# Last output projection on float16 pairs: splits of gated tiles spread over several heads, one stored group per weight block, second half left to the scheduler

## The chip, the cores and the metric

The kernel runs on one core of a Trainium2 chip. The metric is the device time of one execution in microseconds (us), the median of several runs. The engines named here are PE (TensorE, the matrix engine; PEld is its weight load), DVE (VectorE), ACT (ScalarE), POOL (GpSimd) and SP (SyncE, which issues most transfers). Each engine works through its own instruction stream in order; semaphores hold an instruction back until what it needs is there. [...]

## The reference

One step of a streaming encoder of two layers, over 512 prompt tokens and 32 sample tokens (544 rows in all, width 1024). Layer 0 is an RWKV-7 mixer, layer 1 is differential attention with 12 heads; each layer has a gate of 2048 columns and an output projection of 2048 by 1024.

```
h = rmsnorm(x, norm_w)
q, k, v, qm, gate = jnp.split(h @ w_in, [MIX_W, 2 * MIX_W, 3 * MIX_W, 3 * MIX_W + MEM_W], axis=-1)
...                                             # 12 heads of differential attention: o
o = rmsnorm(o, subln) * (1.0 - lam_init)
y_mem = mem_attention(qm, mk, mv)
out = jnp.concatenate([o.reshape(B, T, MIX_W), y_mem], axis=-1) * jax.nn.silu(gate)
return x + out @ w_out, k, v
...
y = rmsnorm(x, final_norm_w)                    # after layer 1
```

Besides `y`, the kernel returns the keys and values of layer 1 and the states of layer 0. The change touches layer 1 alone: the last heads of its attention, and `out @ w_out`.

## The kernel before, in words

Layer 0 takes roughly the first 1000 us and is left as it is. Layer 1 runs one long stream of matrix products on PE. Its unit is a **block**: 128 output columns of a weight matrix, 1024 rows deep. The activations are held as 8 or 16 **tiles** of 128 channels by 544 tokens. A weight block and the activations are both split into a pair of float16 numbers (high part and rest), and a product is the sum of high by high, high by rest and rest by high. A block is thus 2 token halves of 272 by 8 tiles by 3 products: 48 matrix products. The code counts one **step** per product.

**Heads.** The blocks of head h are v, k, q and, for most heads, a gate block; head 11 has four gate blocks. The rest of the attention (scores, softmax, transposes, gating) is a list `ev` of calls in `diff_layer`, each tied to a step number `begin(h) + offset`; when the stream has yielded that many steps, the call is made and its instructions are put in the streams of the engines. The trace places the first steps of heads 8, 9, 10 and 11 at about 1113, 1141, 1162 and 1184 us and the first step of the output projection at 1248.8 us.

**Output projection.** `out` is 16 tiles deep, in two halves. The first 8 blocks (q=0) multiply tiles 0 to 7 by the 8 column blocks of `w_out`; the next 8 blocks (q=1) multiply tiles 8 to 15 and add to the same result. Tiles 0 to 7 are gated during the heads up to 8; tiles 8 to 15 are gated last (tiles 12 to 15 belong to the memory heads). Before a tile can be used it needs a **square** (`gated_square`: ACT squares it and sums along the tokens), then for the whole half a **scale** (`gated_scales`: one small PE product, `ps_gs`, and some DVE work that turns each bound into a power of two), `half_scale` (DVE, the scales that go onto the rows of `w_out`), and a **split** (`gated_split`: ACT writes the high part of `hl`, then DVE the rest).

**Weight blocks.** A weight block passes through a pipeline that `stream` (L1942) places within the steps of the blocks ahead of it. During the products of block i: two loads of 256 KB for block i+4 at steps 1 and 14 (SP issues them; there are four raw buffers `h16s`, so a load waits until the block four before it has been split); two squares of block i+3 on ACT at steps 14 and 27; the column scale of block i+2 at steps 12 to 36 (PE, DVE, then two multiplications on POOL); the split of block i+1 at steps 7, 11, 13 and 17 (ACT casts the high part into `whs`, then POOL subtracts for the first half and DVE for the second). `whs` has two buffers.

**Stored groups.** The attention's keys and values are written to a scratch array in DRAM. Six **groups** (`kv_out`) copy it to the outputs, 1 MB and 64 KB each, DRAM to DRAM, issued by SP. Before, while the first half of the projection runs, a list `left` is worked off one entry every 12 steps: 8 squares, the scales, `half_scale`, 8 splits of tiles 8 to 15; and then, when it is empty, one stored group every 12 steps, at steps 312 to 372 of 768.

**Order.** While `ordered` is set, every instruction is tied behind the one before it on its engine, so the order in the code is the order in the streams. At step 384, when the first half ends, `ordered` is cleared: the Tile scheduler then orders the instructions of the engines by itself, but for those in `tied`, before PE and SP.

**Result.** The sum of a second-half block is added to `x` (`out_add`, L1934). Then the final norm needs a sum of squares over all columns per token (`sums`, `ps_n`), and a transpose of each 128 by 128 piece on PE (`ps_f`) before the rows are stored; the last of this can only be done after the last product.

## Time and profile before

| what | us |
|---|---|
| median of 3 runs (lowest to highest) | 1384.32 (1384.22 to 1386.17) |
| profiled execution | 1382.54 |
| its span (first to last instruction) | 1380.7 |
| first product of the output projection | 1248.8 |
| last product ends | 1369.9 |

The profile is of one execution; every engine's instructions stand in it with start, length and what they waited for. Nearly all instructions are recorded in one helper, so they all bear its line (L133 before, L137 after the change, since four lines are added above it); they are told apart by the names of tiles. A row of a timeline gives the start, the length, the engine, the operation, output and inputs, the shape, a count, and in brackets the idle time of the engine just before and what ended it. A table by windows gives for each stretch the busy time of each engine, the granted PE clock (1.00 is full speed), the mean busy share of the DMA engines, and GB/s. The prediction shows the rows that it uses.

### The profile page before, as it was taken

The page shows a single profiled execution, that of the slowest core. Times are in us where ns is not written, and L with a number is a line of the kernel's source. Part 1 is how long each engine was busy: PE and PEld are TensorE (multiplying, and loading weights), DVE is VectorE, ACT ScalarE, POOL GpSimd, SP SyncE. Part 2 cuts the span into 40 slices and gives each one's busy share as a digit, 9 for nine tenths or more (in the row PEclk, how much of TensorE's full clock was granted, in tenths as well). Part 3 has the DMA queues.
Part 4 walks back from the last instruction along what each step waited for, and adds up shares of the span by engine and source line. Part 5 has one row for each costly group of instructions (what it writes and reads, how often), then busy time and mean ns, then how long its engine had stood idle before and what let it go on. Part 6 is the DMA issues. An engine that isn't in the chain of part 4 may idle for free. (4 is left out here: it accounts for less than half of the span.)

```text
span 1380.7 us, 32358 instructions
## 1 busy us (share of the span) xinstructions
PE 1305.1 (95%) x11775; PEld 1174.1 (85%) x11775; DVE 946.2 (69%) x2475; ACT 888.8 (64%) x2412; POOL 674.0 (49%) x1145
## 2 busy tenths in 40 slices
PE   6999999999999999899999999999999999989776
PEld 6898899999999999888899988888878877868665
DVE  7776777788778777856764464566796679767444
ACT  7665678677877786655643366776766767865442
POOL 2227575557655765540120047565566655535441
PEclk9999999999999999999999999999999999999989
DMA  7542223322332223233284446777777878743711
GB/s 235 176 129 71 67 56 89 97 61 67 93 87 69 72 78 81 58 101 117 60 265 151 129 123 156 184 165 178 171 179 151 185 154 183 162 109 93 254 48 66
DMA packets 418298, 171.55 MB, mean 124 GB/s; under 512 B 195209, under 2 KB 402578, under 8 KB 418138
## 3 DMA queue, kind: packets, MB, share of 16 engines
q1 hardware_dynamic: 417994, 168.96, 47.4%
q8 instruction: 93, 1.52, 0.5%
q14 instruction: 67, 0.55, 0.1%
q10 hardware_dynamic: 144, 0.52, 0.1%
HBM read 130.84 MB, written 41.92 MB: 125 GB/s over the span
## 5 line engine op out<-in xcount | busy, mean ns | idle before, releaser
L133 PEld LDWEIGHTS <-whs 128*128 128x128 f16 x3456 | 330.3, 99 | 85.9 <-ACT whs L133 11.6
L133 PE MATMUL ps_g<-h,whs 128*128 128x272 f16 x2688 | 335.1, 281 | 4.4 <-POOL whs L133 4.4
L133 PE MATMUL ps_g<-hh,wlo 128*128 128x272 f32 x912 | 277.8, 305 | 1.3 <-DVE wlo L133 1.3
L133 PE MATMUL ps_g<-hh,whi 128*128 128x272 f32 x912 | 275.2, 302 | 0.8 <-ACT hh L133 0.8
L133 PE MATMUL ps_g<-hl,whi 128*128 128x272 f32 x912 | 271.4, 298 | 0.6 <-POOL hl L596 0.5
L885 POOL TENSOR_TENSOR tm<-u,m 102x84 f32<-102x84 f32 (+23 forms) x372 | 152.8, 411 | 168.6 <-DMA m<-sc 140.6
L133 POOL TENSOR_TENSOR whs<-h16s,whs 128x512 f16<-128x512 f32 x128 | 150.7, 1195 | 72.2 <-ACT whs L133 70.5
L133 PEld LDWEIGHTS ps_g<-hh,whi 128*128 128x128 f32 x912 | 174.8, 192 | 4.3 <-ACT hh L133 1.2
L133 PEld LDWEIGHTS ps_g<-hh,wlo 128*128 128x128 f32 x912 | 174.0, 191 | 4.6 <-DVE wlo L133 1.9
L133 PEld LDWEIGHTS ps_g<-hl,whi 128*128 128x128 f32 x912 | 174.2, 191 | 2.4 <-POOL hl L596 0.7
L887 POOL TENSOR_TENSOR u<-u,tm 102x84 f32<-102x84 f32 (+23 forms) x372 | 160.0, 430 | 29.1
L133 DVE TENSOR_TENSOR wlo<-raw,whi 128x512 fp32r<-128x512 f32 x178 | 129.3, 736 | 47.7 <-ACT whi L133 46.6
L133 ACT CAST whi<-raw 128x512 fp32r<-128x512 f32 x178 | 107.0, 616 | 35.4 <-issue 19.3
L133 POOL TENSOR_SCALAR h16s<-h16s 128x512 f32<-128x512 f32 x112 | 78.8, 715 | 98.5 <-DVE h16s L133 92.5
L133 PE MATMUL ps_g<-hl,whs 128*128 128x272 f16 x768 | 94.9, 283 | 12.1 <-ACT whs L133 11.3
L133 ACT CAST whs<-h16s 128x512 f16<-128x512 f32 x144 | 84.1, 618 | 31.9 <-POOL h16s L133 26.5
L133 ACT ACTIVATE junkw<-h16s 128x512 bf16<-128x512 f32 x138 | 86.5, 627 | 22.7 <-DMA h16s<-in_w_out_dram 19.5
L133 DVE SCALAR_TENSOR_TENSOR SB<-ps_c,dl,sd 64x64 f32<-64x64 f32 x168 | 47.4, 282 | 42.6 <-PE ps_c L133 38.6
L133 PE MATMUL ps_g<-lo,whi 128*128 128x272 f32 x256 | 73.9, 289 | 0.7 <-DVE lo L133 0.7
L133 PE MATMUL ps_g<-hi,whi 128*128 128x272 f32 x256 | 73.7, 288 | 0.0
L133 PE MATMUL ps_g<-hi,wlo 128*128 128x272 f32 x256 | 73.6, 288 | 0.0
L133 ACT COPY sv<-ps_c 64x64 f32<-64x64 f32 x192 | 39.2, 204 | 38.8 <-PE ps_c L133 36.9
(413 smaller groups left out, 2931.5 us busy)
## 6 DMA issues: line engine op xcount, KB each, us to landing
raw<-in_rw_in_dram SPq DMA_DIRECT2D x114, 256.0 KB
h16s<-in_df_in_dram SPq DMA_DIRECT2D x112, 256.0 KB
raw<-in_w_out_dram SPq DMA_DIRECT2D x32, 256.0 KB
h16s<-in_w_out_dram SPq DMA_DIRECT2D x32, 256.0 KB
ptr<-pk SPq DMA_DIRECT2D x44, 160.0 KB
aT<-ptr SPq DMA_DIRECT2D x11, 640.0 KB
scr<-sg SPq DMA_DIRECT2D x96, 68.0 KB
out_dram<-scr SPq DMA_DIRECT2D x6, 1024.0 KB
```

The lines of the kernel that those rows point to most:

```text
L133: return lambda *a, **k: self.trunk.tie(self, issue(*a, **k))
L885: nc.gpsimd.tensor_tensor(tm[:, :n, :wd], u3[:, :n, kx : kx + 1].to_broadcast(sh), m3[:, kx : kx + 1, kx + 1 :].to_broadcast(sh), ALU.mult)
L887: nc.gpsimd.tensor_tensor(u3[:, :n, kx + 1 :], u3[:, :n, kx + 1 :], tm[:, :n, :wd], ALU.add)
```

## The change

Three things change, all in layer 1.

**Gated tiles 0 to 7.** Before, their squares stood at heads 10 and 11, the scales at step 60 of head 11, and their splits in head 11, with ACT's and DVE's part issued together. Now the squares stand from head 8 to head 10, the scales come in two groups of four (at heads 9 and 10), and the splits stand from step 37 of head 10 on. The rest (DVE's part) is a call of its own, `gated_rest`, 11 steps behind the cast.

**Gated tiles 8 to 15 and the stored groups.** The list in the projection's first half now gives each entry a step of its own. Squares are due from step 24 every 12 steps, but the loop that looks at the list starts at about step 93, so the first six squares are made at once. The scales are due at 126 (they were made at 192), the splits every 24 steps from 150 (they stood every 12 steps from 216), each rest 10 steps later, and the six stored groups every 48 steps, one block, from 164 to 404.

**The second half's order.** `tied` keeps SP alone: PE's order after step 384 is now the scheduler's too.

```diff
+GSQUARE = ((8, 36), (8, 132), (9, 36), (9, 84), (10, 2), (10, 29), (10, 53), (10, 75))
+GSCALE = ((9, 132), (10, 92))
+KVOUT = 164
+GSPLIT, GREST = (37, 66, 84, 115, 134, 180, 227, 252), 11
...
-        x, s = self.o1[g][:], self.out["s"][:, g : g + 1]
-        self.ae.activation(both[:, 0], x, AF.Copy, scale=s)
-        self.ve.scalar_tensor_tensor(both[:, 1], x, s, both[:, 0], ALU.mult, ALU.subtract)
+        self.ae.activation(both[:, 0], self.o1[g][:], AF.Copy, scale=self.out["s"][:, g : g + 1])
         tiles[g] = both[:, 0], both[:, 1]
+
+    def gated_rest(self, g, tiles):
+        hi, lo = tiles[g]
+        self.ve.scalar_tensor_tensor(lo, self.o1[g][:], self.out["s"][:, g : g + 1], hi, ALU.mult, ALU.subtract)
...
-            left = [(self.gated_square, (12, 13, 14, 15, 8, 9, 10, 11)), (lambda g: self.gated_scales(8, 8), (8,)), (self.half_scale, (1,)),
-                    (lambda g: self.gated_split(g, po, tiles), (12, 13, 14, 15, 8, 9, 10, 11))]
-            left = [(fn, g) for fn, gs in left for g in gs]
+            order = (12, 13, 14, 15, 8, 9, 10, 11)
+            left = [(24 + 12 * i, self.gated_square, g) for i, g in enumerate(order)]
+            left += [(126, lambda g: self.gated_scales(g, 8), 8), (138, self.half_scale, 1)]
+            left += [(150 + 24 * i, lambda g: self.gated_split(g, po, tiles), g) for i, g in enumerate(order)]
+            left += [(160 + 24 * i, lambda g: self.gated_rest(g, tiles), g) for i, g in enumerate(order)]
+            left += [(KVOUT + 48 * i, lambda i: kv_out[i](), i) for i in range(len(kv_out))]
+            left.sort(key=lambda x: x[0])
             for _ in main:
                 n += 1
-                if n % 12 == 0:
-                    if left:
-                        fn, g = left.pop(0)
-                        fn(g)
-                    elif kv_out:
-                        kv_out.pop(0)()
+                while left and left[0][0] <= n:
+                    _, fn, g = left.pop(0)
+                    fn(g)
                 if n == KT * 6 * KT:
-                    self.ordered, self.tied = False, (self.te, self.se)
+                    self.ordered, self.tied = False, (self.se,)
...
-            if h >= 10:
-                at(f + 36, lambda h=h: [self.gated_square(g) for g in ((0, 1), (6, 7))[h - 10]])
-                at(f + 66, lambda h=h: [self.gated_square(g) for g in ((2, 3, 4, 5), ())[h - 10]])
-                if last:
-                    at(f + 60, lambda: self.gated_scales(0, 8))
-                    at(f + 70, lambda: self.half_scale(0))
-                    for g in range(8):
-                        at(f + (84, 104, 124, 144, 184, 226, 260, 296)[g], lambda g=g: self.gated_split(g, we[0], tiles))
+                for g, off in enumerate(GSPLIT):
+                    at(f + off, lambda g=g: self.gated_split(g, we[0], tiles))
+                    at(f + off + GREST, lambda g=g: self.gated_rest(g, tiles))
+        for g, (h, off) in enumerate(GSQUARE):
+            at(begin(h) + off, lambda g=g: self.gated_square(g))
+        for g, (h, off) in zip((0, 4), GSCALE):
+            at(begin(h) + off, lambda g=g: self.gated_scales(g, 4))
+        at(begin(11) + 40, lambda: self.half_scale(0))
```

On SP, in the first half of the output projection (`h16s` is half a weight block, `scr` a group's scratch with its two transfers): before,

```order
L133 DMA h16s<-in_w_out_dram 128x4x128 x20
L133 DMA out_dram<-scr_12366 512x512
L133 DMA out_dram<-scr_12366 32x512
L133 DMA out_dram<-scr_12367 512x512
L133 DMA out_dram<-scr_12367 32x512
L133 DMA out_dram<-scr_14354 512x512
L133 DMA out_dram<-scr_14354 32x512
L133 DMA h16s<-in_w_out_dram 128x4x128
L133 DMA out_dram<-scr_14355 512x512
```

and now

```order
L137 DMA h16s<-in_w_out_dram 128x4x128 x14
L137 DMA out_dram<-scr_12366 512x512
L137 DMA out_dram<-scr_12366 32x512
L137 DMA h16s<-in_w_out_dram 128x4x128 x2
L137 DMA out_dram<-scr_12367 512x512
L137 DMA out_dram<-scr_12367 32x512
L137 DMA h16s<-in_w_out_dram 128x4x128 x2
L137 DMA out_dram<-scr_14354 512x512
```

Three groups stood in a row ahead of half a block, and the other three followed with single halves between them; now each group has the two halves of one block behind it.

On ACT, around the third block of the projection (`junkw` from `og` is the square of a gated tile, `whs` the cast of a weight block): before,

```order
L133 ACTIVATE junkw_18711,outt_12363<-og12_12341 128x544
L133 CAST whs_18713<-h16s_11842 128x512
L1874 DMA fw_18704<-in_final_norm_w_dram 128x1024
L133 ACTIVATE junkw_18729,outt_12363<-og13_12342 128x544
L133 CAST whs_18713<-h16s_11842 128x512
L133 ACTIVATE junkw_18739,h16s_11842<-h16s_11842 128x512
L133 ACTIVATE junkw_18752,outt_12363<-og14_12343 128x544
```

and now

```order
L137 ACTIVATE junkw_18712,outt_12363<-og12_12341 128x544
L137 ACTIVATE junkw_18714,outt_12363<-og13_12342 128x544
L137 ACTIVATE junkw_18716,outt_12363<-og14_12343 128x544
L137 ACTIVATE junkw_18718,outt_12363<-og15_12344 128x544
L137 ACTIVATE junkw_18720,outt_12363<-og8_12337 128x544
L137 ACTIVATE junkw_18722,outt_12363<-og9_12338 128x544
L137 ACTIVATE junkw_18727,outt_12363<-og10_12339 128x544
L137 CAST whs_18729<-h16s_11842 128x512
L1881 DMA fw_18708<-in_final_norm_w_dram 128x1024
L137 ACTIVATE junkw_18745,outt_12363<-og11_12340 128x544
L137 CAST whs_18729<-h16s_11842 128x512
```

Seven squares now stand ahead of the first cast of that block, where one stood, and the last square stands ahead of the second cast; the small product `ps_gs` needs all eight.

On DVE, in head 11 (`qp` is the query, `hl` the rest of a gated tile, `snm` the maximum of a row of scores, `pt` the softmax, `ot` the head's output): before,

```order
L133 STREAM_TRANSPOSE pk<-pt 128x512
L133 SCALAR_TENSOR_TENSOR qp<-ps_g,h16s,qp 64x272 x2
L133 SCALAR_TENSOR_TENSOR hl_18001<-og_12332,outs,hl_18001 128x544
L133 TENSOR_SCALAR h16s<-dv,h16s 128x1
L133 TENSOR_TENSOR ot<-ps_o,os_16826 128x512
L133 MEMSET ps_s 64x64 x2
L133 TENSOR_REDUCE snm<-ps_s 128x1 x2
```

and now

```order
L137 STREAM_TRANSPOSE pk<-pt 128x512
L137 SCALAR_TENSOR_TENSOR qp<-ps_g,h16s,qp 64x272 x2
L137 TENSOR_SCALAR h16s<-dv,h16s 128x1
L137 TENSOR_TENSOR ot<-ps_o,os_16830 128x512
L137 MEMSET ps_s 64x64 x2
L137 TENSOR_REDUCE snm<-ps_s 128x1 x2
```

The rest of a gated tile no longer stands between the query and the head's output there.

On PE the small products `ps_gs` move with the scales, and in the second half of the projection the transposes `ps_f` move. After block 11, twenty of them stood in a row; now they stand as groups of 8, 4, 4 and 4 (8, then 4 products, 4, then 1, 4, then 4, 4). In the last three token halves, two groups of 6 transposes and one of 2 stood between the products, the one of 2 with the first norm products (`ps_n`) ahead of the last 48 products. Now they stand as 4, 2, 2, 4 and 2 with 2 to 31 products between them, and the first `ps_n` stand ahead of the last 37 products. After the last product, three `ps_n` and then six `ps_f` remained before; now, six `ps_f` and then three `ps_n`.

## The prediction

> **What bounds the kernel now.** I read the page first, for the span, then the busy times by windows over layer 1's end, then PE's waits there, then SP's transfers and the chain of waits through the longest wait. The page gives

> ```profile
> span 1380.7 us, 32358 instructions
> ```

> against an execution of 1382.54 us, so 1.84 us lie outside the span. The windows cover the output projection (columns: window, its length, busy us of PE, PEld, DVE, ACT and POOL with counts, PE clock, DMA share, GB/s):

> ```profile
> 1249.00:1303.00 54.00, 53.25 (x486) 44.53 (x483) 38.69 (x94) 31.48 (x77) 29.55 (x26) 1.00 0.53 166
> 1303.00:1314.00 11.00, 0.00 (x0) 0.00 (x0) 0.00 (x0) 2.63 (x8) 0.00 (x0) 0.65 0.71 228
> 1314.00:1321.00 7.00, 6.31 (x34) 4.13 (x35) 2.61 (x7) 2.53 (x8) 3.19 (x3) 0.58 0.27 77
> 1321.00:1370.00 49.00, 41.69 (x362) 34.04 (x360) 26.38 (x69) 16.21 (x36) 17.75 (x16) 1.00 0.13 44
> 1370.00:1380.70 10.70, 1.51 (x12) 1.30 (x12) 4.52 (x14) 2.48 (x4) 0.00 (x0) 0.71 0.32 112
> ```

> PE is full in the first half, then has no product at all for 11 us, then runs at a clock of 0.58, then is short of 7.3 us of work in the last 49. PE's waits from 1184 on (what waited, for what; us in total, times, longest) say on whom:

> ```profile
> PE ps_sc L133 <- ACT pt L133: 3.1, 1, 3.1
> PE ps_aT L133 <- DVE pt L133: 2.1, 2, 1.8
> PE ps_aT L133 <- DVE os L133: 1.3, 1, 1.3
> ...
> PE ps_g L133 <- ACT whs L133: 11.3, 1, 11.3
> ...
> PE ps_n L133 <- DVE sums L133: 3.3, 2, 1.7
> PE ps_f L133 <- DVE og L133: 2.9, 2, 1.7
> PE ps_f L133 <- DVE h16s L133: 1.6, 1, 1.6
> PE ps_f L133 <- DVE x L133: 0.9, 2, 0.5
> PE ps_g L133 <- POOL whs L133: 0.8, 2, 0.6
> ```

> The long one names a cast on ACT. ACT itself waited, for a weight load, and the chain of waits leads past that load to the stored groups:

> ```profile
> 1312.05 0.63 ACT L133 ACTIVATE junkw<-h16s 128x512 bf16<-128x512 f32 x1 [6.67 <-DMA h16s<-in_w_out_dram]
> ```

> ```profile
> 1291.71 12.40 DMA out_dram<-scr
> 1304.18 8.61 DMA h16s<-in_w_out_dram
> ...
> 1315.84 4.32 DMA h16s<-in_w_out_dram
> ...
> 1323.45 3.23 DMA h16s<-in_w_out_dram
> ...
> 1329.74 3.18 DMA h16s<-in_w_out_dram
> ```

> SP's timeline shows the six groups as 12 transfers, the first here, and the last before 1302.24:

> ```profile
> 1285.24 5.10 SPq L133 DMA_DIRECT2D out_dram<-scr  x6
> ...
> 1302.24 13.97 SPq L133 DMA_DIRECT2D h16s<-in_w_out_dram  x4
> ```

> So the groups run from 1285.24 to 1304.1 almost without a pause. With two halves of a block among them that is 6 x 1.114 MB + 0.52 MB = 7.2 MB in 18.9 us, an estimated 2.9 us for a group. The weight load of 1304.18 waited behind all of it; PE used up what it had and stood still. That is the bound that the change meets.

> **The change part by part.** A step's length first:

> ```profile
> 1264.10 2.94 PE L133 MATMUL ps_g<-hl,whs 128*128 128x272 f16 x24
> 1266.88 0.19 PE L133 MATMUL ps_g<-h16s 128*128 128x1 bf16 x2
> 1266.93 2.94 PE L133 MATMUL ps_g<-hl,whs 128*128 128x272 f16 x24
> ```

> 24 products per 2.83 us, 0.118 us a step, 5.66 us a block.

> (1) **Groups spread.** One group per block puts 0.52 + 1.11 MB into 5.66 us, 289 GB/s, where the burst moved 7.2 MB in 18.9 us, 380. A load is issued when the split of the block four before it is done (step 17 at the latest) and is squared in the next block from step 14 on; less the time of the split itself some 80 steps lie between, 9.4 us. A load of 3.2 to 4.3 us with a group of 2.9 us ahead of it lands after 6.1 to 7.2. It is hidden. The 11.3 us go, and the slow clock behind them: 6.31 us busy at 0.58 lose 6.31 x 0.42 = 2.65. Against it stands the loop that the second half runs once the scheduler orders it (the square of a later block is put ahead of a cast, so load, square, cast and subtraction follow each other): from 1315.84 to 1323.45 and to 1329.74 it took 7.6 and 6.3 us, more than a block. Four loops of 6.3 lose 2.5; I estimate 0.5 in hand at its start, and 0.8 is waited already (the last row of the waits): +1.2. Sum -12.75, from -14 (no loop) to -7 (two loads late by a group each).

> (2) **Transposes after block 11.** Twenty stood in a row and waited 1.6 + 2.9 = 4.5 us on a chain through DVE, POOL and ACT that the change leaves. Between the first and the last of them now stand 9 products, 9 x 0.118 = 1.06. I take -1.1, nearest to what PE has to put in; ends 0 and -4.5.

> (3) **The last blocks.** The two waits on x (0.9) and the earlier of the two on sums (3.3 - 1.7 = 1.6) now have products ahead of them: up to -2.5. I take -2.0, since the last ones are released late anyhow; ends 0 and -2.5. What follows the last product, 10.7 us, stays.

> (4) **Head 11.** Here the head's output waited behind the rest of a gated tile:

> ```profile
> 1212.01 1.31 DVE L133 SCALAR_TENSOR_TENSOR hl<-og,outs,hl 128x544 f16<-128x544 f32 x1
> ...
> 1213.47 0.69 DVE L133 TENSOR_TENSOR ot<-ps_o,os 128x512 f32<-128x512 f32 x1
> ```

> ```profile
> 1212.00:1216.00 4.00, 0.91 (x37) 0.70 (x36) 3.45 (x8) 1.81 (x7) 0.73 (x1) 1.00 0.88 137
> 1216.00:1220.00 4.00, 2.23 (x13) 1.39 (x12) 3.05 (x10) 2.22 (x9) 1.36 (x2) 0.68 0.89 218
> 1220.00:1224.00 4.00, 4.00 (x21) 2.96 (x20) 0.83 (x5) 2.58 (x9) 2.27 (x2) 0.50 1.09 278
> ```

> Without that 1.31 the wait on pt falls from 3.1 to 1.8, and the next (1.8) by perhaps 0.1: -1.4. Between the two waits the clock fell: 2.23 x 0.32 + 4.00 x 0.50 = 2.7 us lost. With less idle time I expect no fall: -4.1 in all. Ends: 0, the chain is late for another reason; -7.6, both waits gone too.
> [...]

> (5) **The wait on os** (1.3) had a split's rest ahead of it on DVE too, and no split stands there now: -1.0; ends 0 and -1.3.

> (6) **Heads 8 to 10** take the work over. The squares and splits of head 10 (last two rows: all splits of the projection, ns shortest/median/longest):

> ```profile
> 1162.00:1184.00 22.00, 21.28 (x182) 18.38 (x183) 16.64 (x48) 18.30 (x52) 10.94 (x11) 1.00 0.62 139
> ```

> ```profile
> 1261.16 0.64 ACT L133 ACTIVATE junkw<-og 128x544 bf16<-128x544 f32 x1
> 1261.71 0.19 ACT L133 ACTIVATION_READ_ACCUMULATOR junkw<-og 128x1 bf16 x1
> ```

> ```profile
> L133 ACT ACTIVATE hl<-og,outs x16: 732/740/762, 1198.1 to 1288.7; 128x544 f16<-128x544 f32 x16
> L133 DVE SCALAR_TENSOR_TENSOR hl<-og,outs,hl x16: 769/785/1306, 1198.9 to 1289.5; 128x544 f16<-128x544 f32 x16
> ```

> A square takes 0.74 us. Head 10 loses two squares and gains five splits: ACT 18.30 - 1.5 + 3.7 = 20.5 of 22 us, DVE 16.64 + 3.9 = 20.6. PE is full there (21.28 of 22), and ACT and DVE feed it: this work is hidden behind its products as long as both keep ahead, and what they deliver late PE waits for. I take +1.0; ends 0 and +4 (five casts of 0.74 all in the way).

> (7) **A new wait.** `ps_gs` now stands at step 126 and needs all eight squares, which are issued together. On ACT one ended at 1261.9; six more at 0.74, the cast of a weight block (0.53 until the next starts) and the last square end at about 1267.6. PE reaches step 126 some 18 products after the mark of 1264.05, at 1266.2. In-order, PE's products queue behind it: +1.4, ends 0 and +3 (the row it is nearest to is this count itself). The weight cast behind seven squares is late by up to 5, too, but its products come after the wait.

> (8) **Splits of tiles 8 to 15** stand one per 24 steps instead of 12, 0.74 + 0.79 us each, ahead of the weight casts of four blocks: +0.5, ends 0 and +1.5 (one split for each pair of blocks).

> Sum: -12.75 - 1.1 - 2.0 - 4.1 - 1.0 + 1.0 + 1.4 + 0.5 = -18.05. The profiled execution becomes 1364.5, and with the 1.8 by which the median lies above it, **1366.3 us**.

> **The rivals.**
> Better cover: the loop never lags, the transposes and the last waits vanish, and `ps_gs` finds its squares ready. (1) -14, (2) -4.5, (3) -2.5, no (7): -24.6, **1359.7**. For it: every one of these waits is on a chain that runs ahead of PE. Against: 9 products don't cover 4.5 us.
> Head 11 stays: its wait comes from the softmax, and the clock falls as before; (4) is 0: **1370.4**. For it: 1.8 us of the first wait are not explained by the split. Against: the rest is exactly one instruction in order.
> The stall is ACT's order, not the groups: the square that waits at 1312.05 stands ahead of the cast in either kernel. If it keeps the cast back without any burst, (1) is 0: **1379.1**. Against: its load waited 8.61 us where 3.2 is usual, just behind the burst.
> Slower: each of six weight blocks waits for its group. PE would wait 2.9 us six times and lose some 2.7 us of clock each time as in head 11, 33.6 in all: -18.05 + 33.6, **1399.9**. It decides if a load lands more than 9.4 us after its issue; 6.1 to 7.2 by the rows speak against it.
> No effect: the scheduler puts the second half back as it was, and the loads are late for another reason: **1384**.

> **How the numbers follow.** Forecast 47%, better cover 17%, head 11 stays 22%, ACT's order 6%, slower 5%, no effect 3%. A measurement of this kernel tells about 0.2% (2.8 us) from no change, so the first four are faster: 0.92; same 0.03; slower 0.05. The forecast's own range is 1361 to 1371. Head 11's case lies in it, and better cover takes the low end to 1357; (6) and (7) at their upper ends add 4.6 to the case with head 11: 1375. Outside lie the last three cases and tails of the others, 2 in 10.

> **What would show it.** (1) SP alternates groups and pairs of halves, no wait on whs above 1 us near the border, clock 1.00 throughout; wrong if ACT's square before the second half's casts still waits for a load. (2), (3) waits of `ps_f` near 3.4 in all, and one `ps_n` wait, at the end. (4) `ps_sc` waits 1.8 us and the clock stays at 1.00. (6) new waits on ACT or DVE between 1113 and 1184. (7) `ps_gs` waits for `junkw`, 1 to 2 us. The prediction is wrong if the groups' transfers lengthen loads beyond 9 us, or if head 10's full engines cost PE more than (4) and (5) bring.

## The result, and the profile after

The changed kernel takes 1365.55 us (median of 4 runs, 1361.0 to 1367.86) against 1385.24 before (4 runs beside them): a ratio of 0.985 (0.982 to 0.989), 19.7 us. A second set of executions gave 1364.33 against 1384.88. The forecast was 1366.3.

The profiled execution took 1367.86 us, with a span of 1366.0, 14.7 us below the span before. PE's waits in the changed kernel, first for the heads (1095 to 1249 us), then from there to 1300, then to the end (what waited for what; us in total, times, longest):

```profile
PE ps_s L137 <- ACT pt L137: 2.3, 1, 2.3
PE ps_s L137 <- DMA kh<-kh: 2.1, 1, 2.1
PE ps_oT L137 <- DVE og L137: 1.7, 1, 1.7
PE ps_aT L137 <- DVE pt L137: 1.1, 1, 1.1
...
PE ps_gs L137 <- ACT junkw L137: 0.6, 1, 0.6
...
PE ps_g L137 <- POOL whs L137: 2.2, 3, 0.8
PE ps_f L137 <- DVE og L137: 2.0, 2, 1.2
PE ps_f L137 <- DVE h16s L137: 1.4, 1, 1.4
PE ps_g L137 <- ACT whs L137: 1.0, 1, 1.0
PE ps_n L137 <- DVE sums L137: 0.5, 1, 0.5
PE ps_f L137 <- DVE x L137: 0.5, 2, 0.3
```

The wait of 11.3 us for a cast is down to 1.0, with 2.2 beside it for POOL's part. Of head 11's waits the ones on scores (`ps_sc`, 3.1) and on os (1.3) are gone, and the one of `ps_aT` on `pt` is 1.1 where it was 1.8. The `ps_gs` wait that was forecast is there with 0.6. New are 2.3 us in head 11's first block and 1.7 in head 10's. SP's timeline shows the groups between the halves of weight blocks:

```profile
1267.87 1.25 SPq L137 DMA_DIRECT2D out_dram<-scr  x2
1271.99 1.56 SPq L137 DMA_DIRECT2D h16s<-in_w_out_dram  x2
1273.60 1.17 SPq L137 DMA_DIRECT2D out_dram<-scr  x2
1278.41 1.40 SPq L137 DMA_DIRECT2D h16s<-in_w_out_dram  x2
```

A table that a single profile's waits can't give was worked out from the starts of PE's products in each trace: how long PE took for stretches of 48-product blocks. Block 0 is the first of the projection, block 8 the first of its second half, and negative numbers are the blocks of the heads (-7 is head 11's first). The last column ends with the start of the last product. All kernels that the experiments made stand in it, us:

```
kernel                            -14..-5  -4..-1   0..7   8..10  11..13  14,15
before                               77.0    45.7   48.1    31.6    24.9   16.2
changed                              83.8    35.7   48.3    20.4    24.0   13.9
changed, second profile              82.6    37.3   48.3    21.2    24.2   14.0
before, groups spread                76.9    45.4   48.1    22.3    26.2   16.2
changed, groups in a burst           83.8    37.3   48.3    32.7    24.2   14.0
changed, PE tied                     82.4    37.3   48.3    18.8    27.2   16.2
changed, old heads                   76.7    45.6   48.5    22.6    22.5   14.0
changed, groups late                 82.3    37.2   48.3    17.7    23.7   14.0
changed, heads eased                 80.9    37.2   48.3    19.7    24.1   14.0
changed, ACT tied                    80.0    38.9   48.3    17.0    19.4   14.4
changed, burst and ACT tied          80.7    38.9   48.3    21.8    19.4   14.4
changed, eased, ACT tied, late       81.6    37.3   48.3    17.0    19.4   14.4
changed, eased, ACT tied             79.3    37.3   48.3    17.0    19.4   14.4
before, ACT tied                     77.0    44.9   48.1    20.3    20.9   16.6
```

From the start of the last product to the end of the span all of them took 10.9 to 11.2 us. Block -14 began between 1125.0 and 1128.9 us after the span's start; no edit touches layer 0, and blocks -17 to -15, just ahead of block -14, take the same in all kernels, so this difference is not the edits' work. By the same starts, in the kernel before, head 8 begins at 1103.3 us, head 9 at 1135.4 and head 10 at 1156.7, earlier than the 1113, 1141 and 1162 given above. The change's gain is thus 10 to 11 us at the start of the second half (blocks 8 to 10), 8 to 10 in head 11's last four blocks, and 3 in the last five blocks of all, less 6 to 7 that the ten blocks from head 8's last to head 11's third gave back.

### The profile page after: what moved, and what is told of

It reads as the page before. It is cut to its first block, busy times and chain, and to the rows that moved or that the text cites. A ratio compares the mean times of both kernels' runs of the same rounds, so it can differ in the third digit from the quotient of the medians.

```text
span 1366.0 us, 32365 instructions
## 1 busy us (share of the span) xinstructions
PE 1300.2 (95%) x11776; PEld 1170.6 (86%) x11776; DVE 945.2 (69%) x2477; ACT 887.7 (65%) x2412; POOL 679.6 (50%) x1145
## 5 line engine op out<-in xcount | busy, mean ns | idle before, releaser
L889 POOL TENSOR_TENSOR tm<-u,m 102x84 f32<-102x84 f32 (+23 forms) x372 | 159.3, 428 | 165.3 <-DMA m<-sc 134.4
```

What stands on the lines that cost most here:

```text
L889: nc.gpsimd.tensor_tensor(tm[:, :n, :wd], u3[:, :n, kx : kx + 1].to_broadcast(sh), m3[:, kx : kx + 1, kx + 1 :].to_broadcast(sh), ALU.mult)
```

## The experiments

**Groups alone.** The kernel before, with one group per block and nothing else changed:

```diff
-                if n % 12 == 0:
-                    if left:
-                        fn, g = left.pop(0)
-                        fn(g)
-                    elif kv_out:
-                        kv_out.pop(0)()
+                if n % 12 == 0 and left:
+                    fn, g = left.pop(0)
+                    fn(g)
+                if n in range(164, 405, 48):
+                    kv_out.pop(0)()
```

> The kernel before with one part of the change alone: one stored group every 48 steps, at steps 164 to 404, instead of one every 12 from 312. Theory (the groups' burst held the weight load back): the wait of 11.3 us for the cast in the first block of the second half falls below 1.5 us, the slow clock behind it is gone, and the time falls by 11.3 + 2.65 - 1.2 = 12.7 us, to about 1372 (1368 to 1376). Rival (ACT's order keeps the cast back whatever the groups do): the wait stays at 8 us or more and the time at 1385.

Measured: 1374.59 us, a ratio of 0.9934 (0.9914 to 0.9953). Blocks 8 to 10 fell from 31.6 to 22.3 us. PE's waits for the weights are now, in the stretch from block 0 on:

```profile
PE ps_g L133 <- POOL whs L133: 1.7, 2, 0.8
PE ps_g L133 <- ACT whs L133: 1.4, 2, 1.0
```

The longest load in the chain of waits there takes 4.94 us, where it took 8.61. So spreading the groups is enough to end the long wait. In this profile 1.3 of the 9.3 us come back in blocks 11 to 13, with the clock at 0.50 there from 1332.20 to 1339.02 us.

**Burst put back** into the changed kernel:

```diff
-KVOUT = 164
+KVOUT = 312
-            left += [(KVOUT + 48 * i, lambda i: kv_out[i](), i) for i in range(len(kv_out))]
+            left += [(KVOUT + 12 * i, lambda i: kv_out[i](), i) for i in range(len(kv_out))]
```

> The changed kernel with that part undone alone: one stored group every 12 steps from step 312. Theory: loads of the second half wait behind the groups again, PE waits 8 to 11 us for a cast in blocks 8 to 10 and the clock halves there; 1375 to 1379. Rival: no wait above 2 us comes back, 1366.

Measured: 1377.29 us (0.9951, 0.9928 to 0.9975). The wait is back in one piece, in PE's waits:

```profile
PE ps_g L137 <- ACT whs L137: 12.6, 1, 12.6
```

and in ACT's timeline the square of a later block, which stands ahead of the cast, waits for its load:

```profile
1310.98 0.63 ACT L137 ACTIVATE junkw<-h16s 128x512 bf16<-128x512 f32 x1 [7.67 <-DMA h16s<-in_w_out_dram]
...
1312.37 1.12 ACT L137 CAST whs<-h16s 128x512 f16<-128x512 f32 x2
```

Both experiments agree with the theory of the groups. Neither excludes that the burst does it only through ACT's order, which the scheduler sets in both; that is tried below.

**PE tied** in the second half again:

```diff
-                    self.ordered, self.tied = False, (self.se,)
+                    self.ordered, self.tied = False, (self.te, self.se)
```

> The changed kernel with PE tied in the second half, as before. Theory: twenty transposes stand in a row again, and the norm's products too; blocks 11 to 15 take 3 us more together (1.1 for the first transposes, 2.0 in the last blocks), 1368 to 1369. Rival (the weight loop alone sets the pace of blocks 9 to 15, so PE has slack either way): within 0.5 us in those blocks.

Measured: 1370.29 us (0.9899, 0.9883 to 0.9915). Blocks 11 to 13 take 27.2 instead of 24.2 and blocks 14 and 15 16.2 instead of 14.0. They lose 5.2 together, more than the 3 forecast, and the rival (within 0.5) is out. Blocks 8 to 10 took 18.8 instead of 21.2, so that the whole second half lost 2.8. This need not come from PE's order: the first load of the chain of waits there took 4.49 us, against 5.50 in the changed kernel's first profile, and it took 4.48 in "heads eased" below, where PE is not tied and blocks 8 to 10 took 19.7. The waits are those of the kernel before, with 2.4 for 2.9 on `og`:

```profile
PE ps_n L137 <- DVE sums L137: 3.3, 2, 1.7
PE ps_f L137 <- DVE og L137: 2.4, 2, 1.2
PE ps_f L137 <- DVE h16s L137: 1.6, 1, 1.6
```

**Old heads**: squares, scales and splits of tiles 0 to 7 where they stood before.

```diff
-                for g, off in enumerate(GSPLIT):
-                    at(f + off, lambda g=g: self.gated_split(g, we[0], tiles))
...
+            if h >= 10:
+                at(f + 36, lambda h=h: [self.gated_square(g) for g in ((0, 1), (6, 7))[h - 10]])
+                at(f + 66, lambda h=h: [self.gated_square(g) for g in ((2, 3, 4, 5), ())[h - 10]])
...
+                        at(f + (84, 104, 124, 144, 184, 226, 260, 296)[g],
+                           lambda g=g: (self.gated_split(g, we[0], tiles), self.gated_rest(g, tiles)))
```

> The changed kernel with squares, scales and splits of tiles 0 to 7 where they stood before (heads 10 and 11). Theory: the waits of 3.1 and 1.8 us in head 11 come back, and the wait of 2.3 us at head 11's first block goes; by the two profiles blocks -4 to -1 (the last four of the heads) take 9.9 us more and the blocks before them 6.6 less, of which 2 to 3 halvings of the clock at 1.7 us are chance; so 1367 to 1371. Rival (the heads' new schedule costs as much as it brings): 1365 to 1366.

Measured: 1369.26 us (0.9895, 0.9876 to 0.9914). The heads' two stretches are those of the kernel before, 76.7 and 45.6, and its waits in head 11 too:

```profile
PE ps_sc L137 <- ACT pt L137: 3.1, 1, 3.1
PE ps_aT L137 <- DVE pt L137: 2.1, 2, 1.8
PE ps_aT L137 <- DVE os L137: 1.3, 1, 1.3
```

So the new heads bring 8.3 in their last four blocks and cost 5.9 in the ten ahead of them: a net 2.4 us in these profiles. The medians are 3.7 to 4.9 us apart.

**The changed kernel again**, on the chip of the next three.

> The changed kernel itself, on the same chip as the three below, as their base and to see what varies from one execution to the next. Expected: the block times of the projection as in its first profile to 0.1 us; the heads' blocks differ where a clock halving falls elsewhere; 1362 to 1368.

Measured: 1364.33 us (1362.32 to 1367.74). Blocks 0 to 7 repeat to 0.1 us. Blocks 8 to 10 don't: 21.2 against 20.4, so the forecast of 0.1 us fails there, where PE waits behind transfers.

**Groups late**, behind the last weight load:

```diff
-KVOUT = 164
+KVOUT = 548
-            left += [(KVOUT + 48 * i, ...
+            left += [(KVOUT + 24 * i, ...
```

> The changed kernel with the six stored groups behind the last weight load (issued from step 548 on, all in a row). Theory (a group on its way lengthens the loads of blocks 11 and 12 from 3.2 to 5.5 and 4.8 us, and the loop of load, square, cast and subtraction passes that on): those loads take 3.2 to 3.5, PE's waits for whs fall from 3.2 us to 1.5 or less, 1.5 to 2.5 us less than the changed kernel. Rival (the loop alone sets the pace): no difference above 0.5 us in blocks 8 to 13.

Measured: 1361.84 us (0.984, 0.980 to 0.988). Blocks 8 to 10 fell to 17.7. The chain of waits has the loads of the second half first in the changed kernel, then with late groups:

```profile
1295.82 5.50 DMA h16s<-in_w_out_dram
...
1304.37 4.77 DMA h16s<-in_w_out_dram
...
1312.43 3.11 DMA h16s<-in_w_out_dram
```

```profile
1292.07 3.08 DMA h16s<-in_w_out_dram
1298.21 4.40 DMA h16s<-in_w_out_dram
1305.67 3.00 DMA h16s<-in_w_out_dram
1311.73 2.95 DMA h16s<-in_w_out_dram
```

The windows of the first two loads of the changed kernel, and of the second one with late groups (the last number is GB/s):

```profile
1295.82:1301.32 5.50, 5.50 (x53) 4.64 (x52) 1.46 (x6) 2.14 (x8) 2.04 (x2) 1.00 0.91 304
1304.37:1309.14 4.77, 4.77 (x47) 4.04 (x45) 1.36 (x6) 1.15 (x3) 2.04 (x2) 1.00 0.40 113
```

```profile
1298.21:1302.61 4.40, 4.40 (x42) 3.71 (x41) 1.36 (x6) 1.15 (x3) 2.04 (x2) 1.00 0.43 123
```

The theory holds for one of its two loads. In the first, 304 GB/s over 5.50 us are 1.67 MB, a block and a group, and without the group it took 3.08 us. In the second, 113 GB/s over 4.77 us are 0.54 MB, the block alone, and with late groups it still took 4.40; what makes it longer than the 3 us of those behind it is open. In blocks 8 to 10 the late groups are worth 1 to 3.5 us against the four profiles of kernels with new heads, one group per block and ACT left to the scheduler (18.8 to 21.2). The medians differ by 2.5 us, which their intervals don't tell from nothing. And with short loads, too, the chain still goes from load to load: the loop is there.

**Heads eased**: two calls moved by some steps.

```diff
-GSQUARE = ((8, 36), (8, 132), (9, 36), ...
+GSQUARE = ((8, 36), (8, 144), (9, 36), ...
-                    at(f + off + GREST, lambda g=g: self.gated_rest(g, tiles))
+                    at(f + off + (24 if g == 4 else GREST), lambda g=g: self.gated_rest(g, tiles))
```

> The changed kernel with two calls moved by some steps: DVE's rest of tile 4 behind the row maxima of head 11's first scores (24 steps behind its cast, not 11), and the square of tile 1 from step 132 to 144 of head 8, behind the query on ACT. Theory (these two stand in front of the chain that PE waits for): block -7 falls from 9.4 to about 7 us, block -14 from 11.5 to 9.2 with no clock halving there; 3 to 5 us less than the changed kernel. Rival (waits only move on to the next consumer): under 1 us.

Measured: 1364.53 us, no difference from the changed kernel that the times tell, where 3 to 5 us less were forecast. Block -7 took 8.2 us and block -14 11.2. In the changed kernel the row of DVE that the theory blames, the maximum behind it and PE's wait:

```profile
1194.91 1.15 DVE L137 SCALAR_TENSOR_TENSOR hl<-og,outs,hl 128x544 f16<-128x544 f32 x1
...
1196.29 0.49 DVE L137 TENSOR_REDUCE snm<-ps_s 128x1 f32<-128x128 f32 x2
```

```profile
1197.12 0.39 PE L137 MATMUL ps_s<-kh,qp 128*128 128x256 f32 x1 [2.33 <-ACT pt L137]
```

and with the two calls moved:

```profile
PE ps_s L137 <- DMA kh<-kh: 2.0, 1, 2.0
...
PE ps_s L137 <- ACT pt L137: 1.2, 1, 1.2
```

The wait in block -7 fell by 1.1, about the length of the instruction that stood ahead; the other half of it is from something else. The wait on `kh` hardly moved (2.1 and 2.3 in the two profiles of the changed kernel), so the square was not its cause. Block -14 took 8.9 to 9.2 us in the four profiles with old heads, 9.1 to 9.8 in three with new ones and 11.2 to 12.9, with a halved clock, in seven (0.50 for 3.41 us, from 1133.66 us in the changed kernel, 1129.22 with the burst put back and 1131.60 with PE tied). Its wait on `kh` was 1.1 to 1.4 us with old heads, and with new ones 1.9 to 2.5 in nine profiles and 1.4 in one; what makes the difference is open.

**ACT tied** in the second half, PE, DVE and POOL left to the scheduler:

```diff
-                    self.ordered, self.tied = False, (self.se,)
+                    self.ordered, self.tied = False, (self.se, self.ae)
```

> The changed kernel with ACT kept in the written order in the second half (PE, DVE and POOL left to the scheduler), so that a cast stands ahead of the square of a later block as in the first half. Theory (the squares put ahead make the loop): waits for whs fall from 3.2 to below 1 us and blocks 8 to 10 to 5.7 to 6 us each; 2 to 3 us less. Rival (the loads' own time sets the pace): unchanged; or the sums of the norm, now in order too, hold casts back and it is slower by 1 to 3 us.

Measured: 1360.79 us (0.9821, 0.9779 to 0.9864). The second half is 50.8 us, 8.6 less than in the second profile of the changed kernel: blocks 8 to 10 take 5.66 us each, as in the first half, and no wait for weights is left between 1240 us and the end:

```profile
PE ps_f L137 <- DVE x L137: 0.8, 3, 0.4
PE ps_gs L137 <- ACT junkw L137: 0.6, 1, 0.6
PE ps_n L137 <- DVE sums L137: 0.5, 1, 0.5
PE ps_oT L137 <- DVE og L137: 0.2, 1, 0.2
```

The second half's products took 57.8 to 59.4 us in three profiles with ACT's order left to the scheduler (the changed kernel twice, and heads eased), so this edit brings 7.0 to 8.6 there. The medians are only 3.5 us apart (1364.33 and 1360.79; 2 to 3 were forecast), and the profile used for the changed kernel was the slowest of its four executions; the pair with heads eased, below, is 7 us apart by its ratios.

The waits of the transposes for `og` and `h16s` went too (3.4 to 0). In the changed kernel, just ahead of them, DVE had waited for ACT's cast:

```profile
1323.37 1.23 DVE L137 TENSOR_TENSOR whs<-h16s,whs 128x512 f16<-128x512 f32 x1 [1.56 <-ACT whs L137]
```

That their chain ran over this cast, behind squares that waited for loads, fits the rows and is not shown by a run of its own.

**Burst and ACT tied**, the case that parts the two causes: both edits above in one kernel.

> The changed kernel with the groups in a burst again (one every 12 steps from step 312) and ACT kept in the written order in the second half. It tells whether the burst alone makes the wait of block 8, or only together with ACT's order. Theory (burst alone: a load behind 18.9 us of transfers is late by more than the 9.4 us in hand): a wait of 6 to 10 us for whs in blocks 8 to 10 remains; about 1370. Rival (both are needed; with casts ahead of later squares only the square of a block two further on is late): PE waits 2 us or less there, and the time is that of the kernel with ACT tied, 1361.

Measured: 1361.0 us (0.9837, 0.9823 to 0.985). The wait of 12.6 us is not there; what is left is

```profile
PE ps_g L137 <- ACT junkw L137: 2.7, 3, 1.0
```

On ACT a square waits for its load as before, but the cast that PE needs next has been made ahead of it:

```profile
1302.22 1.12 ACT L137 CAST whs<-h16s 128x512 f16<-128x512 f32 x2
1308.11 0.63 ACT L137 ACTIVATE junkw<-h16s 128x512 bf16<-128x512 f32 x1 [4.77 <-DMA h16s<-in_w_out_dram]
```

The load itself was as late as with the burst alone, 9.81 us in the chain of waits against 10.47. Blocks 8 to 10 take 21.8 instead of 32.7 (17.0 without the burst). The rival was right, but for a wait of 2.7 us where it said 2 or less: with casts first the burst costs 4.8 us there, the 2.7 and 1.7 in the 24 products from 1309.85 us, which took 4.61 us where 24 took 2.94 just before; 0.4 is left over. The long wait needed both.

**Before, ACT tied**: the same one word in the kernel before, with its burst and its PE order.

```diff
-                    self.ordered, self.tied = False, (self.te, self.se)
+                    self.ordered, self.tied = False, (self.te, self.se, self.ae)
```

> The kernel before with one edit: ACT too kept in the written order in the second half (groups in their burst, PE tied as before). Theory (the wait of 11.3 us needs the burst and ACT's order together): blocks 8 to 10 fall from 31.6 to about 22 us, and with the norm's sums in order too 1371 to 1375. Rival (in this kernel the burst alone is enough, since its splits of tiles 8 to 15 end later): blocks 8 to 10 stay above 28 us, 1382 or more.

Measured: 1369.84 us (0.9909, 0.989 to 0.9927). Blocks 8 to 10 fall from 31.6 to 20.3, 11 to 13 from 24.9 to 20.9; the late load takes 9.98 us in the chain of waits, and the long wait is gone all the same. What is left of PE's waits for ACT in the second half is

```profile
PE ps_g L133 <- ACT junkw L133: 2.9, 3, 1.3
```

One word brings 13.5 us, where the whole change brings 19.7, with the groups still in a burst.

**Together**: ACT tied and heads eased, with the groups late or one per block.

> The changed kernel with three edits together: ACT kept in the written order in the second half, the groups behind the last load, and the two calls in heads 8 and 11 moved. Theory (the loop is gone with ACT's order, so late groups bring nothing more): blocks 8 to 15 within 0.3 us of 50.8 in all, block -7 at 8.2; 1359 to 1360. Rival (groups and order each bring their part): 2 us better than that.

> As the kernel above with the groups where the changed kernel has them, one per block. Theory: the same time as above to 1 us, 1359 to 1360. Rival (groups under way still cost): 1 to 2 us slower than above.

Measured: 1354.8 us (0.9796, 0.9776 to 0.9816) and 1355.9 us (0.9802, 0.9789 to 0.9816), the same within their intervals, as the theory had it. Blocks 8 to 15 take 50.8 in both and block -7 takes 8.2, as forecast; the times are 3 to 5 us better than it said, and why is open. They are 28.5 and 27.4 us below the kernel before. The second ratio lies 0.005 below that of heads eased alone (0.9853), which is 7 us.

## Why the prediction was right, and where it was not

The sum was -18.05 us and the medians moved by 19.7 and 20.6. The terms, against the second profile of the changed kernel, where the heads have one stretch at half clock fewer (the first profile's, 3.41 us at 0.50 from 1198.51, falls in block -6 and moves 1.5 us from head 11's last four blocks to the row of (6)):

| step | forecast | measured |
|---|---|---|
| (1) groups spread, blocks 8 to 10 | -12.75 | -10.4 (first profile -11.2) |
| (2) transposes, blocks 11 to 13 | -1.1 | -0.7 |
| (3) last blocks | -2.0 | -2.2 |
| (4), (5) head 11 | -5.1 | -8.4 (first profile -10.0) |
| (6) heads 8 to 10, and 11's start | +1.0 | +5.6 (first profile +6.8) |
| (7), (8) first half | +1.9 | +0.2 |

These add up to -15.9. The medians moved 4 us more. The profiled execution before lay 1.8 to 2.7 us below the medians of its kernel, the two after 2.3 and 3.4 above theirs, and where the clock halves differs from one execution to the next, in layer 0 too (between 200 and 320 us it does at 311.05 in the first profile of the changed kernel and at 263.27 in the second); that this is all of the 4 us is argued, not shown.

(1) was right in place and near in size, and wrong in what it took for sufficient. The step that failed is the count of 9.4 us in hand, and with it the rejection of "ACT's order": that rival was weighed as one cause or the other. The 9.4 us reach to the square of the load, but the long wait of PE is for a cast of an earlier block. It needed a late load *and* a square of that load put ahead of the cast that PE needs next. The load was late in all four kernels with the burst: it took 8.61 and 10.47 us where ACT's order is the scheduler's, 9.81 and 9.98 with casts first. PE's wait for ACT in the second half was 11.3 and 12.6 us in the former two, 2.7 and 2.9 in the latter. Groups spread or casts first, either ends it.

The loop's term was mis-sized as well: it was put at 1.2 us of lag, and against casts in order the second half loses 7.0 to 8.6 us to ACT's order. The sign that the prediction named for being wrong here, an ACT square ahead of the second half's casts that still waits for a load, is in the changed kernel's profile:

```profile
1300.58 0.63 ACT L137 ACTIVATE junkw<-h16s 128x512 bf16<-128x512 f32 x1 [3.34 <-DMA h16s<-in_w_out_dram]
...
1301.96 1.12 ACT L137 CAST whs<-h16s 128x512 f16<-128x512 f32 x2
```

(2) and (3): the waits of `ps_f` came to 3.9 us where 3.4 were forecast, and one `ps_n` wait is left, as forecast. The -0.7 of (2) holds the loop's cost in blocks 11 to 13 too; putting PE's order back alone costs 3.0 there and 2.2 in the last blocks.

(4) and (5): the wait on scores fell from 3.1 to 0.5 or 0 where 1.8 was forecast, the next, on `pt`, was 1.8 or 1.1 where 1.7 was, and the wait on os (1.3) is gone. Why the first fell so far is open. The new wait of 2.3 us in head 11's first block stands ahead of it, but with 1.1 us of that taken away (heads eased) the wait on scores did not grow again; it was 0.4. That the clock would not fall, 2.7 of the 4.1 us, was the author's estimate, which no run shows by itself. The halved clock of the kernel before (0.50 from 1217.48 to 1224.31 us) is gone in both profiles of the changed kernel. That is partly chance: two stretches of 3.41 us at 0.50 stood there in all four profiles with old heads, none in eight of the ten with new ones, and one in the other two (ACT tied: from 1219.21). Their sum was short by 3 to 5.

(6) is the term that was most off, past its upper end of 4. It priced the added work by ACT's and DVE's share of head 10. But 2.9 us of it fell in block -7, and 1.2 of these came from one instruction of 1.15 us in front of a row maximum, the same kind of thing whose removal (4) counted as a gain 20 us later. The order of DVE's instructions holds both. Another 2.2 to 2.5 fell in block -14, 0.6 to 0.9 of it wait, and in both profiles a halved clock; the cause of that wait is open.

(7): the wait was forecast at 1.4 and measured at 0.6; block 2 lost 0.8 us, and blocks 1 and 3 gained 0.7. (8) did not show.

The result was near by luck: against the sum, (1) was worse by 2.4 us and (6) by 4.6, (4) and (5) were better by 3.3 and (7) and (8) by 1.7.

## What to carry to other kernels

A long wait can have two causes that are both necessary; undoing one shows that it matters, not that the other does not, and only the run with one cause back and the other gone tells. When an engine is left to a scheduler, look at what the scheduler puts ahead of the instruction that the bound engine needs next: an early step of a later block that waits for a transfer turned a prefetch into a loop here, at 7.0 to 8.6 us. And work moved out of one head must be looked up in the order where it lands, instruction by instruction, not by that engine's share of busy time.

## What the runs showed of the hardware

```profile
1130.25:1133.66 3.41, 1.35 (x11) 0.90 (x9) 1.98 (x7) 1.75 (x7) 1.36 (x2) 1.00 0.96 216
1133.66:1137.07 3.41, 3.29 (x17) 2.38 (x17) 2.38 (x12) 2.26 (x8) 2.27 (x2) 0.50 0.94 236
1137.07:1140.48 3.41, 3.41 (x32) 2.91 (x30) 3.07 (x16) 1.10 (x3) 1.36 (x2) 1.00 1.14 334
```

The window with 1.35 us of PE work is followed by one at half speed, and that one, with PE busy for 3.29 us, by one at full speed. In layer 1 of the two profiles, each of the six stretches at 0.50 stands behind a window in which PE was busy for 0.00 to 1.51 us of 3.41 (before: 1.31 from 1214.07 us, 0.00 from 1302.81, 1.51 from 1371.08; changed: 1.35 from 1130.25, 1.39 from 1195.10, 1.41 from 1355.53). A window with 1.48 us (before, from 1210.65) has one at full speed behind it. With PE tied one with 1.75 us (from 1128.19) is followed by 0.50 and one with 1.76 (from 1189.63) by 1.00, so PE's busy time alone does not tell them apart. In layer 0 the clock was also at 0.50 behind windows that were full by this measure (at 446.07 and 538.23 us in the kernel before, with PE busy for 3.35 and 3.36 us of the window ahead), which these runs don't explain.

Waits of the same length in head 11 (1.8 us on `pt`, and 0.4 or 0.5 on scores) had a window at full speed behind them in one run and a halved one in another: with the heads eased PE was busy for 1.65 us from 1216.30 and the next window was at 1.00; with ACT tied it was busy for 1.51 us from 1215.80 and the next was at 0.50. Blocks -4 to -1 took 37.2 us in the former and 38.9 in the latter. Nor was every halved window paid for. In the changed kernel's first profile one lay in block -6 (from 1198.51 us), which took 8.0 us against 6.5 in the second; the wait in block -4 was shorter there, 10.2 us against 11.7, and the sum of the two blocks is the same. Single executions of one kernel spread over 2 to 12 us; how much of that comes from the clock is not shown.
